# Stationary activation tiles moved to ten byte offsets against the streamed weights

## The chip, the core and the metric

One core of one Trainium2 chip runs the whole program. The metric is device time in microseconds (us), the median of several executions. The two activations and the products below run on the matrix engine (PE in the profile); its weight loads are shown apart, as PEld. DVE is the vector engine, ACT the scalar engine, POOL and SP two further engines; SP issues the transfers of the weights.

## What is computed

A decoder trunk of two layers on one sequence of 256 positions and width 2048, in float32. Layer 0 is sparse attention and a gated feed-forward, layer 1 a pooling mixer and a second gated feed-forward. The change touches the operands of three products: both down projections and the output product of the mixer.

```python
def pool_mixer(h, w_in, w_grp, scale, w_out):
    ...
    mixed = jnp.einsum('bsgc,gcd->bsgd', pooled, w_grp.astype(jnp.float32)).reshape(B, S, D)
    mixed = (mixed * scale.astype(jnp.float32)).astype(h.dtype)
    return mixed @ w_out

def swiglu(h, w_gu, w_down):
    gu = h @ w_gu
    gate, up = gu[..., :D_FF], gu[..., D_FF:]
    return (jax.nn.silu(gate) * up) @ w_down
```

D_FF is 5632, so a down projection has 44 blocks of 128 along its contraction; the mixer's output product has 16.

## The kernel before

Every float32 operand is kept as two parts, a rounded one and the rest. Weights arrive in blocks of 128 partitions by 1024 elements (`wraw`), in the order of one list, and ACT (L137) and DVE (L138) split each into `whi` and `wlo`; three buffers of each are in flight. An activation tile of 128 partitions holds 256 positions of the rounded part and 256 of the rest, side by side.

The large products are all made by `wide_gemm`. For each block k of the contraction, and each half t of the positions, it issues three matmuls. The activations `xa`, `xb` (128 by 128) are the stationary operand, loaded into the array by a weight load of its own, and 512 columns of `whi` or `wlo` are the moving operand:

```python
            for t in range(2):
                xa, xb = (rhs[k][:, a * S + t * P:a * S + (t + 1) * P] for a in range(2))
                nc.tensor.matmul(ps[t], xa, hi, start=k == 0, stop=False)
                nc.tensor.matmul(ps[t], xa, lo, start=False, stop=False)
                nc.tensor.matmul(ps[t], xb, hi, start=False, stop=k == n - 1)
```

These are lines 214 to 216. What the title of a row calls `acc<-whi,hid` is such a matmul: `whi` streams, `hid` stands in the array. The stationary tiles are `oT` (attention output, 16 tiles), `xg` (the normed input, 16), `hid` (the gated activation, 44, in 22 pairs, once in each feed-forward) and `mixed` (the mixer's, 16). A down projection runs four column blocks j, and in each of them all 44 blocks k in order.

In `ffn` the gate and up products alternate; ACT and DVE make `h` from them (L741, L745), PE transposes `h` (L752), and `split_pair` writes a pair of `hid` tiles (ACT L730, DVE L731). `mix_group` multiplies `pooled` by small weights and writes `mixed` (L815, L816). The weights' split waits for PE to free a buffer; nothing is ordered by hand around the change.

**Where the tiles lie.** Pools are stacked from the low end of the memory of a partition, their tiles one after another, each rounded up to a multiple of 32 bytes. The pool of `whi`, `wlo` and `wraw` begins 96 bytes past a multiple of 256, and its eleven buffers have 4096 bytes, so every streamed block lies at 96 modulo 256. `xg` follows directly: the same place. Between `xg` and the pool of the feed-forward lie 32 bytes for `rcol`, six times 32 for `na`, `nt` and `tot`, 32 for `ssq`, and tiles of 1024, 2048 and 16384 bytes: the small ones add up to 256, and `hid` lies at 96 again. In front of `mixed` lie tiles of 6144, 6144, 256 and eight times 4096 bytes: 96 too. `oT` is in a pool that is filled from the high end, and lies at 224, which is 128 bytes off the streamed blocks. In the text "off" is the place of a stationary tile minus that of the streamed one, modulo 256. The parts of a tile used by `wide_gemm` begin at multiples of 512 bytes in it, and those of a streamed block at 0 or 2048, so they add nothing to it.

Of the kernel before, what the change touches and what calls it, by code (L numbers as in the profile page):

```python
# [11 lines left out]
F32 = mybir.dt.float32  # L12
F32R = mybir.dt.float32r
# [4 lines left out]
P = 128  # L18
D = 2048
S = 256  # L20
KC = D // P
# [10 lines left out]
FT = DFF // P  # L32
# [35 lines left out]
def nsa_pool_trunk(ctx, tc, first, xn, small, band, gfin, w_qk, w_vg, w1k, w1v, w_o,  # L68
# [135 lines left out]
    def wide_gemm(rhs, own=False):  # L204

        ps = [bank(own) for _ in range(2)]
        n = len(rhs)
        for k in range(n):
            if k % 2 == 0:
                w = next_block()  # L210
            hi, lo = (a[:, k % 2 * N5:(k % 2 + 1) * N5] for a in w)
# [5 lines that stand above are left out]
        return ps  # L217
# [60 lines left out]
    at = ctx.enter_context(ExitStack())  # L278
# [17 lines left out]
    with tc.tile_pool(name="first", bufs=1, reuse_waits="tile") as fp, \  # L296
# [13 lines left out]
        for k in range(KC):  # L310
            n = wx[k].shape[1]
            o = KC + k * XW if k else 0
# [7 lines left out]
            for a, b in ((0, P), (P, F1)) if k == 0 else ((0, F1),):  # L320
                t = wx[k][:, n - F1 + a:n - F1 + b]
# [45 lines left out]
        f = rst.rearrange("p (c m j) -> p c m j", m=KQ, j=4)  # L367
# [13 lines left out]
        f = rst.rearrange("p (c i k) -> p i c k", i=CS // 2, k=2)  # L381
        for j in range(2):
            ps = ps1[3 + j].rearrange("p (c i k) -> p i c k", i=CS // 2, k=2)
            for g in range(2):
                a = slice(g * DV, (g + 1) * DV)
                o = (2 * j + g) * CS
# [17 lines left out]
        for br in range(2):  # L404
# [4 lines left out]
            for u in range(2):  # L409
                o = CS + u * S + br * P  # L410
# [240 lines left out]
    for q in range(NH // 4):  # L651
# [8 lines left out]
        for h in range(4 * q, 4 * q + 4, 2):  # L660
# [7 lines left out]
            o = oT[h // 2]  # L668
# [17 lines left out]
    def row_scale():  # L686

        tot = tmp.tile([P, 2], F32, name="tot")
        a = tmp.tile([P, 2], F32, name="na")
        t = tmp.tile([P, 2], F32, name="nt")  # L690
        nc.vector.tensor_reduce(tot, ssq, axis=AX.X, op=OP.add)
        nc.scalar.activation(t, tot, AF.Sqrt, scale=1.0 / D, bias=eps)
        nc.vector.tensor_scalar(a, tot, 1.0 / D, EPS, op0=OP.mult, op1=OP.add)
        nc.vector.reciprocal(rcol, t)
        nc.vector.scalar_tensor_tensor(t, rcol, -0.5, rcol, op0=OP.mult, op1=OP.mult)
        nc.vector.tensor_tensor(t, t, a, op=OP.mult)
        nc.vector.scalar_tensor_tensor(rcol, t, 1.5, rcol, op0=OP.add, op1=OP.mult)
# [22 lines left out]
            for i in range(2):  # L720
                spread(4 * j + 2 * q + i, tr[:, i * S:(i + 1) * S], gain)

    def pairs(pool, n, name):

        both = [pool.tile([P, 2, 2 * S], F32R, name=f"{name}{i}") for i in range(n // 2)]
        return both, [both[c // 2][:, c % 2] for c in range(n)]

    def split_pair(dst, tr):
# [1 line left out]
        nc.scalar.activation(dst[:, :, :S], src, AF.Copy)  # L730
        nc.vector.tensor_tensor(dst[:, :, S:], src, dst[:, :, :S].bitcast(F32), op=OP.subtract)  # L731

    def ffn(gain, fpool):
        hid2, hid = pairs(fpool, FT, "hid")
        for f in range(FJ):
            pg = wide_gemm(xg)
            if f == 0:
                row_scale()
            sg = [fpool.tile([P, N5], F32, name=f"sg{t}", bufs=1) for t in range(2)]
            for t in range(2):  # L740
                nc.scalar.activation(sg[t], pg[t], AF.Silu, scale=rcol[:, t:t + 1])  # L741
            pu = wide_gemm(xg)
            h = [fpool.tile([P, N5], F32, name="h", bufs=4) for t in range(2)]
            for t in range(2):
                nc.vector.scalar_tensor_tensor(h[t], pu[t], rcol[:, t:t + 1], sg[t], op0=OP.mult,  # L745
                                               op1=OP.mult)
            for q in range(2):
                tr = turn()
                for i in range(2):
                    for t in range(2):  # L750
                        o = (2 * q + i) * P
                        nc.tensor.transpose(tr[:, i * S + t * P:i * S + (t + 1) * P],  # L752
                                            h[t][:, o:o + P], ident)
                split_pair(hid2[2 * f + q], tr)
        gf = None
        if gain is None:
            gf = [fpool.tile([P, N5], F32, name="h", bufs=4) for _ in range(NJ)]
            for j in range(NJ):
                nc.sync.dma_start(gf[j], gfin[:, j * N5:(j + 1) * N5])
        for j in range(NJ):  # L760
            residual(j, wide_gemm(hid), gain, gf)
        return gf
# [3 lines left out]
    op.close()  # L766

    with tc.tile_pool(name="f0", bufs=1, reuse_waits="tile") as fpool:
        ffn("g_mix1", fpool)


    with tc.tile_pool(name="pl", bufs=1, reuse_waits="tile") as pl:

        raw = pl.tile([P, 4, 3 * P], F32, name="raw")
        bh = pl.tile([P, 4, 3 * P], F32R, name="bh")
        bl = pl.tile([P, 4, CS], F32R, name="bl")
        nc.sync.dma_start(raw, band)
        nc.gpsimd.tensor_copy(bh, raw)
        nc.gpsimd.tensor_tensor(bl, raw[:, :, :CS], bh[:, :, :CS].bitcast(F32), op=OP.subtract)
        pooled2, pooled = pairs(pl, KC, "pooled")  # L780
        mixed = [pl.tile([P, 2 * S], F32R, name=f"mixed{c}") for c in range(KC)]

        def pool_group(g, first):
            ps = wide_gemm(xg)
            if first:
                row_scale()
            uh = [pl.tile([P, N5], F32R, name=f"uh{t}", bufs=2) for t in range(2)]
            ul = [pl.tile([P, N5], F32R, name=f"ul{t}", bufs=2) for t in range(2)]
            for t in range(2):
                r = rcol[:, t:t + 1]  # L790
                nc.scalar.activation(uh[t], ps[t], AF.Copy, scale=r)
                nc.vector.scalar_tensor_tensor(ul[t], ps[t], r, uh[t].bitcast(F32), op0=OP.mult,
                                               op1=OP.subtract)
            for q in range(2):
                tr = turn()
                for i in range(2):
                    a = slice((2 * q + i) * P, (2 * q + i + 1) * P)
                    d = tr[:, i * S:(i + 1) * S]
                    nc.tensor.matmul(d, uh[0][:, a], bh[:, g, :S], start=True, stop=False)
                    nc.tensor.matmul(d, ul[0][:, a], bh[:, g, :S], start=False, stop=False)  # L800
                    nc.tensor.matmul(d[:, :CS], uh[0][:, a], bl[:, g], start=False, stop=False)
                    nc.tensor.matmul(d[:, P:], uh[1][:, a], bh[:, g, S:], start=False, stop=False)
                    nc.tensor.matmul(d[:, P:], ul[1][:, a], bh[:, g, S:], start=False, stop=True)
                split_pair(pooled2[2 * g + q], tr)

        def mix_group(g):
            for b in range(2):
                hi, lo = next_block()
                for j in range(2):
                    c = 4 * g + 2 * b + j  # L810
                    ps = bank()[:, :S]
                    for k in range(4):
                        o = (4 * j + k) * P
                        product(ps, hi[:, o:o + P], lo[:, o:o + P], pooled[4 * g + k], k == 0, k == 3)
                    nc.scalar.activation(mixed[c][:, :S], ps, AF.Copy, scale=col("scale", c))  # L815
                    nc.vector.scalar_tensor_tensor(mixed[c][:, S:], ps, col("scale", c),  # L816
                                                   mixed[c][:, :S].bitcast(F32), op0=OP.mult,
                                                   op1=OP.subtract)

        for i, g in enumerate(GROUPS):  # L820
            pool_group(g, i == 0)
            if i:
                mix_group(GROUPS[i - 1])
        mix_group(GROUPS[-1])
        rhs = [mixed[4 * g + c] for g in GROUPS for c in range(4)]
        for j in range(NJ):
            residual(j, wide_gemm(rhs), "g_ffn1")

    with tc.tile_pool(name="f1", bufs=1, reuse_waits="tile") as fpool:
        gf = ffn(None, fpool)  # L830
        row_scale()
        for j in (*range(NJ - 1), NJ - 1):
            for t in range(2):
                o = xs[:, t, j * N5:(j + 1) * N5]
                r = rcol[:, t:t + 1]
                if j == NJ - 1:
                    nc.vector.scalar_tensor_tensor(o, o, r, gf[j], op0=OP.mult, op1=OP.mult)
                elif t:
                    nc.scalar.activation(o, o, AF.Copy, scale=r)
                else:  # L840
                    nc.vector.tensor_scalar(o, o, r, None, op0=OP.mult)
                nc.sync.dma_start(out[t * P:(t + 1) * P, j * N5:(j + 1) * N5], o)
# [124 lines left out]
```

## Time and profile before

| | us |
|---|---|
| median of three runs | 2141.97 |
| lowest and highest | 2141.78, 2144.75 |
| the profiled execution | 2139.86 |
| span of its trace | 2137.7 |
| mean granted clock of PE, share of full speed | 0.997 |

The span runs from the first to the last instruction; the 2.2 us between it and the execution's time lie around it. All durations below come from this one execution, which is 2.1 us under the median. The page gives shares of the span by engine and a chain of the work that ended last; the other views are lists of groups of instructions, windows of time, and the instructions in order of time. Matmuls overlap in the pipeline, so the duration of one (some 390 ns) is more than what it adds: what counts here is the distance from the start of one matmul to the start of the next, called the pitch.

### The profile page before, as it was taken

The page shows a single profiled execution, that of the slowest core. Times are in us where ns is not written, and L with a number is a line of the kernel's source. Part 1 is how long each engine was busy: PE and PEld are TensorE (multiplying, and loading weights), DVE is VectorE, ACT ScalarE, POOL GpSimd, SP SyncE. Part 2 cuts the span into 40 slices and gives each one's busy share as a digit, 9 for nine tenths or more (in the row PEclk, how much of TensorE's full clock was granted, in tenths as well). Part 3 has the DMA queues.
Part 4 walks back from the last instruction along what each step waited for, and adds up shares of the span by engine and source line. Part 5 has one row for each costly group of instructions (what it writes and reads, how often), then busy time and mean ns, then how long its engine had stood idle before and what let it go on. Part 6 is the DMA issues. An engine that isn't in the chain of part 4 may idle for free.

```text
span 2137.7 us, 28134 instructions
## 1 busy us (share of the span) xinstructions
PE 2114.5 (99%) x10826; PEld 1807.7 (85%) x10826; DVE 1182.7 (55%) x1544; ACT 1036.8 (48%) x1491; POOL 53.2 (2%) x103
## 2 busy tenths in 40 slices
PE   8999999999999999999999999999999999999997
PEld 8999999888888888888888888888888888888886
DVE  7768888554554445544445555555444554444443
ACT  6567777454444444444444455444444444444443
POOL 1001111000000000000000000000000000000000
PEclk9999999999999999999999999999999999999999
DMA  6764444666666666666666655666666666666664
GB/s 231 216 211 136 150 141 132 198 183 191 191 184 195 188 190 193 183 193 188 196 189 190 197 177 178 187 188 187 190 191 189 189 187 193 189 208 194 193 193 127
DMA packets 113960, 396.92 MB, mean 186 GB/s; under 512 B 13314, under 2 KB 17538, under 8 KB 113570
## 3 DMA queue, kind: packets, MB, share of 16 engines
q1 hardware_dynamic: 113634, 394.80, 61.4%
q8 instruction: 85, 1.39, 0.3%
q10 hardware_dynamic: 192, 0.33, 0.1%
q14 instruction: 49, 0.40, 0.1%
HBM read 391.25 MB, written 2.16 MB: 184 GB/s over the span
## 4 chain that ended last, share of the span: by engine, by line
PE 93%; DVE 0%; ACT 0%; DVEq 0%; issue 0%
PE acc L214 27%; PE acc L215 27%; PE acc L216 27%; PE acc L169 2%; PE acc L171 2%; PE acc L170 2%; PE turn L752 1%; PE ps_o L645 1%; PE ps_t L607 1%; PE ps_s L541 1%; PE ps_s L539 1%; PE ps_s L540 1%; PE turn L718 0%; PE ps_o L636 0%; PE ps_o L635 0%; PE ps_o L637 0%
## 5 line engine op out<-in xcount | busy, mean ns | idle before, releaser
L138 DVE TENSOR_TENSOR wlo<-wraw,whi 128x1024 fp32r<-128x1024 f32 (+1 forms) x714 | 874.1, 1225 | 853.6 <-ACT whi L137 847.1
L137 ACT ACTIVATE whi<-wraw 128x1024 fp32r<-128x1024 f32 (+1 forms) x714 | 754.7, 1057 | 918.2 <-PE acc L216 849.9
L216 PE MATMUL acc<-whi,xg 128*128 128x512 f32 x1536 | 599.8, 390 | 0.0
L215 PE MATMUL acc<-wlo,xg 128*128 128x512 f32 x1536 | 598.3, 390 | 0.0
L214 PE MATMUL acc<-whi,xg 128*128 128x512 f32 x1536 | 545.8, 390 | 0.0
L215 PEld LDWEIGHTS acc<-wlo,xg 128*128 128x128 f32 x1536 | 288.4, 188 | 59.5
L216 PEld LDWEIGHTS acc<-whi,xg 128*128 128x128 f32 x1536 | 288.3, 188 | 59.1
L214 PEld LDWEIGHTS acc<-whi,xg 128*128 128x128 f32 x1536 | 288.4, 188 | 58.5
L215 PE MATMUL acc<-wlo,hid 128*128 128x512 f32 x704 | 274.2, 390 | 0.0
L216 PE MATMUL acc<-whi,hid 128*128 128x512 f32 x704 | 274.1, 389 | 0.0
L214 PE MATMUL acc<-whi,hid 128*128 128x512 f32 x704 | 247.5, 390 | 0.0
L214 PEld LDWEIGHTS acc<-whi,hid 128*128 128x128 f32 x704 | 132.1, 188 | 27.4
L216 PEld LDWEIGHTS acc<-whi,hid 128*128 128x128 f32 x704 | 132.1, 188 | 27.4
L215 PEld LDWEIGHTS acc<-wlo,hid 128*128 128x128 f32 x704 | 132.2, 188 | 27.2
L169 PE MATMUL acc<-xg,whi 128*128 128x256 f32 x464 | 131.8, 287 | 0.6 <-ACT whi L322 0.3
L170 PE MATMUL acc<-xg,whi 128*128 128x256 f32 x464 | 131.4, 286 | 0.0
L171 PE MATMUL acc<-xg,wlo 128*128 128x256 f32 x464 | 127.7, 285 | 0.0
L169 PEld LDWEIGHTS acc<-xg,whi 128*128 128x128 f32 x464 | 88.4, 191 | 1.2 <-ACT whi L322 0.6
L170 PEld LDWEIGHTS acc<-xg,whi 128*128 128x128 f32 x464 | 88.4, 190 | 0.2
L171 PEld LDWEIGHTS acc<-xg,wlo 128*128 128x128 f32 x464 | 86.4, 190 | 0.0
L567 ACT ACTIVATE prob<-prob,mx 128x128 f32<-128x128 f32 (+1 forms) x128 | 56.6, 445 | 9.8 <-DVE mx L561 6.8
L215 PE MATMUL acc<-wlo,oT 128*128 128x512 f32 x128 | 50.6, 395 | 0.0
(221 smaller groups left out, 1862.9 us busy)
## 6 DMA issues: line engine op xcount, KB each, us to landing
wraw<-in_gu SPq DMA_DIRECT2D x352, 512.0 KB, 3.6
wraw<-in_down SPq DMA_DIRECT2D x176, 512.0 KB, 3.7
wraw<-in_w_qk SPq DMA_DIRECT2D x60, 512.0 KB, 4.1
wraw<-in_w_o SPq DMA_DIRECT2D x32, 512.0 KB, 3.6
wraw<-in_p_in SPq DMA_DIRECT2D x32, 512.0 KB, 3.6
wraw<-in_p_out SPq DMA_DIRECT2D x32, 512.0 KB, 3.6
wx<-in_first SPq DMA_DIRECT2D x15, 448.0 KB, 8.9
bias<-skew SPq DMA_DIRECT2D x32, 200.0 KB, 3.3
```

Of the source, the lines that this page charges most:

```text
L137: nc.scalar.activation(hi[:, :n], t[:, :n], AF.Copy)
L138: nc.vector.tensor_tensor(lo[:, :n], t[:, :n], hi[:, :n].bitcast(F32), op=OP.subtract)
L169: nc.tensor.matmul(ps, hi, x[:, :S], start=first, stop=False)
L170: nc.tensor.matmul(ps, hi, x[:, S:], start=False, stop=False)
L171: nc.tensor.matmul(ps, lo, x[:, :S], start=False, stop=last)
L214: nc.tensor.matmul(ps[t], xa, hi, start=k == 0, stop=False)
L215: nc.tensor.matmul(ps[t], xa, lo, start=False, stop=False)
L216: nc.tensor.matmul(ps[t], xb, hi, start=False, stop=k == n - 1)
L539: nc.tensor.matmul(o, q[0], k[0], start=True, stop=False)
L540: nc.tensor.matmul(o, q[0], k[1], start=False, stop=False)
L541: nc.tensor.matmul(o, q[1], k[0], start=False, stop=True)
L567: nc.scalar.activation(p[:, o:o + n], p[:, o:o + n], AF.Exp, bias=mx[:, i:i + 1], accum_out=su[:, i:i + 1])
```

## The change

`pairs`, which allocates the tiles of `hid` and `pooled`, gets a list of wanted offsets in bytes. The pairs are cut into as many groups, in order of k. In front of a group a tile that nobody uses fills up multiples of 32 bytes; what is left under 32 bytes is made inside the tile, which then has 64 elements more. `mixed` gets 64 elements more in each tile and begins 1, 2, 12 or 60 elements into it.

- First feed-forward: `hid` at 64, 160, 192 and 224 bytes off, for 12, 10, 12 and 10 of the 44 blocks k.
- Mixer: `mixed` at 4, 8, 48 and 240 bytes off, four blocks k each.
- Second feed-forward: `hid` at 16 and 128 bytes off, 22 blocks k each.
- `pooled` gets no list and stays where it is. The tiles behind the padding move with it: `h` and `sg` by 224 bytes in the first feed-forward and by 128 (modulo 256) in the second.

No instruction is added or taken away; operands keep their shapes.

```diff
-    def pairs(pool, n, name):
-
-        both = [pool.tile([P, 2, 2 * S], F32R, name=f"{name}{i}") for i in range(n // 2)]
+    def pairs(pool, n, name, lines=()):
+
+
+        both, at = [], 0
+        for i in range(n // 2):
+            want = lines[i * len(lines) // (n // 2)] if lines else 0
+            if (want - at) % 256 // 32:
+                pool.tile([P, (want - at) % 256 // 32 * 8], F32, name=f"off{i}")
+                at = want // 32 * 32
+            fine = want % 32 // 4
+            t = pool.tile([P, 4 * S + (64 if fine else 0)], F32R, name=f"{name}{i}")
+            both.append(t[:, fine:fine + 4 * S].rearrange("p (c s) -> p c s", c=2))
         return both, [both[c // 2][:, c % 2] for c in range(n)]
...
-    def ffn(gain, fpool):
-        hid2, hid = pairs(fpool, FT, "hid")
+    def ffn(gain, fpool, lines):
+        hid2, hid = pairs(fpool, FT, "hid", lines)
...
-        ffn("g_mix1", fpool)
+        ffn("g_mix1", fpool, (64, 160, 192, 224))
...
-        mixed = [pl.tile([P, 2 * S], F32R, name=f"mixed{c}") for c in range(KC)]
+        mixed = [pl.tile([P, 2 * S + 64], F32R, name=f"mixed{c}") for c in range(KC)]
+        mixed = [t[:, o:o + 2 * S] for t, o in zip(mixed, (1,) * 4 + (2,) * 4 + (12,) * 4 + (60,) * 4)]
...
-        gf = ffn(None, fpool)
+        gf = ffn(None, fpool, (16, 128))
```

## Rows read from the trace of the kernel before

**Rows 1.** The page: busy time and share, then the chain that ended last.
```profile
PE 2114.5 (99%) x10826; PEld 1807.7 (85%) x10826; DVE 1182.7 (55%) x1544; ACT 1036.8 (48%) x1491; POOL 53.2 (2%) x103
...
PE 93%; DVE 0%; ACT 0%; DVEq 0%; issue 0%
```

**Rows 2.** Waits of PE, longest: line, releaser: us in total, times, longest.
```profile
PE acc L270 <- DVE rcol L267: 3.0, 1, 3.0
```

**Rows 3.** By tile (hid, mixed, oT): count, duration ns min/median/max, first and last start.
```profile
L214 PE MATMUL acc<-whi,hid x704: 387/389/483, 941.5 to 2123.3; 128*128 128x512 f32 x176
...
L730 ACT ACTIVATE hid<-turn x44: 592/596/599, 502.9 to 1890.2; 128x512 fp32r<-128x512 f32 x44
...
L214 PE MATMUL acc<-whi,mixed x128: 389/389/483, 1304.8 to 1394.0; 128*128 128x512 f32 x128
...
L214 PE MATMUL acc<-whi,oT x128: 390/393/497, 345.4 to 451.7; 128*128 128x512 f32 x128
```

**Rows 4.** Windows: stretch and length, busy us of each engine (instructions), PE clock, DMA share, GB/s.
```profile
414.00:434.00 20.00, 20.00 (x88) 16.21 (x87) 11.04 (x12) 9.19 (x13) 0.00 (x0) 1.00 0.61 176
481.00:501.00 20.00, 20.00 (x90) 16.53 (x90) 9.98 (x10) 8.28 (x8) 0.00 (x0) 1.00 0.67 194
1020.00:1040.00 20.00, 20.00 (x90) 16.57 (x89) 8.72 (x8) 8.22 (x8) 0.00 (x0) 1.00 0.67 189
1321.00:1331.00 10.00, 10.00 (x46) 8.29 (x45) 5.24 (x6) 5.47 (x8) 0.00 (x0) 1.00 0.62 176
```

**Rows 5.** Timeline of PE (start us, duration us): first and last instruction of three windows.
```profile
413.67 0.39 PE L216 MATMUL acc<-whi,oT 128*128 128x512 f32 x1
...
433.88 0.40 PE L216 MATMUL acc<-whi,oT 128*128 128x512 f32 x1
...
1019.76 0.39 PE L214 MATMUL acc<-whi,hid 128*128 128x512 f32 x1
...
1039.93 0.39 PE L214 MATMUL acc<-whi,hid 128*128 128x512 f32 x1
...
1320.68 0.39 PE L215 MATMUL acc<-wlo,mixed 128*128 128x512 f32 x1
...
1330.88 0.39 PE L215 MATMUL acc<-wlo,mixed 128*128 128x512 f32 x1
```

**Rows 6.** Timeline of PE: consecutive matmuls with oT standing.
```profile
416.93 0.39 PE L215 MATMUL acc<-wlo,oT 128*128 128x512 f32 x1
417.15 0.39 PE L216 MATMUL acc<-whi,oT 128*128 128x512 f32 x1
417.38 0.40 PE L214 MATMUL acc<-whi,oT 128*128 128x512 f32 x1
417.62 0.40 PE L215 MATMUL acc<-wlo,oT 128*128 128x512 f32 x1
417.86 0.40 PE L216 MATMUL acc<-whi,oT 128*128 128x512 f32 x1
```

**Rows 7.** Timeline of PE: xg standing, right behind the transposes that end at 458.24.
```profile
458.79 0.40 PE L214 MATMUL acc<-whi,xg 128*128 128x512 f32 x1
459.03 0.40 PE L215 MATMUL acc<-wlo,xg 128*128 128x512 f32 x1
...
461.55 0.39 PE L214 MATMUL acc<-whi,xg 128*128 128x512 f32 x1
461.78 0.39 PE L215 MATMUL acc<-wlo,xg 128*128 128x512 f32 x1
```

**Rows 8.** Timeline of PE, 256 columns: v0h or v0l standing, th or tl streaming.
```profile
228.37 0.28 PE L635 MATMUL ps_o<-th,v0h 128*128 128x256 f32 x1
...
229.31 0.28 PE L637 MATMUL ps_o<-th,v0l 128*128 128x256 f32 x1
```

**Rows 9.** Timeline of PE, 256 columns: whi or wlo standing, pooled streaming.
```profile
1262.01 0.28 PE L171 MATMUL acc<-pooled,wlo 128*128 128x256 f32 x1
...
1263.57 0.28 PE L171 MATMUL acc<-pooled,wlo 128*128 128x256 f32 x1
```

**Rows 10.** By line: transposes of xs (L718) and of h (L752).
```profile
L718 PE MATMUL turn<-ident,xs x96: 270/272/275, 387.0 to 1400.4; 128*128 128x128 f32 x96
...
L752 PE MATMUL turn<-ident,h x176: 270/272/275, 501.7 to 1889.7; 128*128 128x128 f32 x176
```

## Prediction

> **What bounds the kernel now.** I read the page first: PE is busy for 2114.5 of 2137.7 us, and the chain that ended last is PE's for 93%, with nothing of DVE or ACT in it that counts [rows 1]. Then the waits of PE: the longest is one of 3.0 us [rows 2]. So PE never waits for data in the three products that the change touches, and a change of layout can only count through how fast matmuls follow each other. Durations of matmuls don't tell that, since they overlap; the pitch does. I took it in stretches without transposes, from the first and last start in a window and the count of instructions in the window.
>
> - `oT` standing: 413.67 to 433.88 us with 88 matmuls, 20.21 / 87 = 232.3 ns [rows 4, 5].
> - `hid` standing: 1019.76 to 1039.93 us with 90, 20.17 / 89 = 226.6 ns [rows 4, 5].
> - `mixed` standing: 1320.68 to 1330.88 us with 46, 10.20 / 45 = 226.7 ns [rows 4, 5].
> - `xg`: also 90 in 20 us [rows 4].
>
> The instruction, its shape and PE's clock (1.00, so 2.4 GHz) are the same in all four. 512 columns at 2.4 GHz are 213.3 ns, so a matmul pays 13.3 ns on top with `xg`, `hid` and `mixed`, and 19.0 with `oT`. What differs by the program is the place: the first three lie 0 off the streamed weights, `oT` 128 off. This is the row on which everything rests: **a tile 128 bytes off costs 232.3 - 226.6 = 5.7 ns a matmul.** Two more views say how it comes. With `oT` the pitch never settles, it goes 0.22, 0.23, 0.24, 0.24 [rows 6]; with `xg` it is as uneven right behind a break (0.24) and then settles at 0.23 within some ten matmuls [rows 7]. The place 0 off thus seems to be one at which loads and streams fall into step, and the step is a cheap one.
>
> **The change part by part.** No instruction comes or goes. Of `hid`, three lines times 704 matmuls are touched, 2112; of `mixed` three times 128, 384 [rows 3]; 2496 in all. One block k has 4 x 2 x 3 = 24 matmuls. All of them are on the path that sets the end, with no cover: each ns of pitch counts in full.
>
> *Second feed-forward, 22 blocks at 128 off:* 22 x 24 = 528 matmuls. It is `oT`'s place, so 528 x 5.7 ns = 3.0 us.
>
> *First feed-forward, at 64, 160, 192 and 224 off:* 288, 240, 288 and 240 matmuls, 1056 in all. No stretch of the trace has 512 columns at these places. The bounds: from above, each pitch as long as the longest in [rows 6], 0.24 against 0.227, so 13 ns; from below, the shortest there, 0.22, so 7 ns less than now. That below nothing is not excluded is seen in 256-column matmuls: `v0h` and `v0l`, by the allocation 32 off what streams past them, have 0.94 us / 8 = 117.5 ns [rows 8], and weights that stand 0 off `pooled` have 1.56 / 13 = 120.0 [rows 9]. There, being off costs nothing and even saves 2.5 ns. I take the nearest row of the same shape, `oT`: 1056 x 5.7 = 6.0 us, with ends of -7 and +14 us.
>
> *Mixer at 4, 8, 48 and 240 off, and the other half of the second feed-forward at 16 off:* 384 + 528 = 912 matmuls. These lie within 48 bytes of place 0, which costs nothing more, so they stand between two rows: 0 and 5.7. I take the middle, 2.85: 912 x 2.85 = 2.6 us, with the same outer ends, -6 and +12 us.
>
> *Writers and transposes.* ACT's write of `hid` has 596 ns [rows 3] and DVE's like it; they run in engines that are busy for 48 and 55% [rows 1]. If misplaced writes took twice as long, the first product would still find its tile, since a down projection reads k in the order in which `ffn` wrote it and only the last pair is written just ahead of it. I cost them at nothing; without that cover one late pair per feed-forward costs about a write, 0.6 us. `h` moves too, to 224 and 128 off. `xs`, which is transposed in the same way from 224 off, has the same 272 ns as `h` [rows 10]: nothing. Padding adds no DMA and moves none in its queue. Behind each edge between two places some ten matmuls fall into a new step; at some 5 ns each, and 4 x (3 + 3 + 1) edges, that is 1.4 us if all had to; I leave it in the range.
>
> The sum is 3.0 + 6.0 + 2.6 = 11.6 us, on a span of 2137.7 and an execution of 2139.86: 2151.5. The median of runs is 2.1 us higher, so the forecast is 2153.6.
>
> **A rule that speaks against this.** The rows show that a pitch of the same shape differs with the stage by 5.7 ns [rows 4, 5]. The Trainium skill, page "TensorE: Matmul & The Clock Gate", section "Step-by-step: what each phase is for", says that PE has two independent read ports and that loading the next weights takes no read bandwidth from the running matmul. By it no place is better than another, and the sum would be 0. The trace does not bear it out: even 0 off, a matmul pays 13.3 ns over its columns.
>
> **The rivals.**
>
> 1. *Nothing changes.* The 5.7 ns of `oT` belong to its stage, not to its place, and loads and streams don't meet. For it: the 256-column rows, where being off is no dearer [rows 8, 9]; and that stretch has DVE busy for 11.0 of 20 us against 8.7 with `hid` [rows 4]. Against: `mixed` has DVE at 5.24 of 10 us, as busy, and the DMA share of `oT`'s stretch, and yet 226.7 ns [rows 4, 5]. Price 0: 2142. That the padding doesn't move what it means to move would give about the same: the places made inside the tiles, 4 to 240 and 16, stay, at 2.6 us or less. Chance 0.15.
> 2. *Faster.* The mechanism is the same falling into step, but at some places the step is shorter than 0 off's. The point from which it decides: the unknown 1968 matmuls must save more than the 3.0 us at 128 off cost, 1.5 ns each. For it: single pitches of 0.22 [rows 6] and the 256-column rows. Against: in 87 pitches with `oT` the short ones are paid back by 0.24s. At the 256-column gain of 2.5 ns, 1968 x 2.5 = 4.9 us less the 3.0: 2140. At 7 ns it is 13.8 less 3.0: 2131. Chance 0.07.
> 3. *Every place but 0 costs what 128 costs, also the near ones.* 2496 x 5.7 = 14.2 us: 2156. It differs from the forecast only in the near places and counts with it.
> 4. *Places that are no multiple of 16 or 32 bytes off cost far more*, since a load then touches more of the memory's lines. If 4, 8, 48, 240 and 16 took the longest pitch of [rows 6], 912 x 13 = 12 us in place of 2.6: 2163. Chance 0.08.
>
> **How the numbers follow.** Forecast with rival 3: 0.70, times from 2146.5 (only `oT`'s place and a third of the others pay) to 2158. Nothing changes 0.15, faster 0.07, far dearer 0.08. The range that leaves two in ten out reaches from 2142 to 2160. A measurement of this kernel tells some 0.2% from no change, 4.3 us: slower is over 2146.3, faster under 2137.7. Rival 2 is half within that band at its small price, so faster gets 0.04; same gets 0.15 from rival 1, 0.03 from rival 2 and 0.02 from the low end of the forecast, 0.20; slower 0.76.
>
> **What the profile after would show.** Windows of the second down projection's later half of each j: 88 instead of 90 matmuls in 20 us, and starts that step 0.22 to 0.24 as in [rows 6]. The first down projection: the same for most of its blocks; a group that stays at 90 has fallen into step at another place. The mixer's product: a pitch between 226.7 and 232. PE's waits, the counts of instructions, and the pitch with `xg` and `oT` stay. The prediction is wrong if the pitch at 128 off stays at 226.7 (then the stage, not the place, made `oT` slow), or if a group falls under 225.

## The result and the profile after

The changed kernel takes 2155.29 us, median of three runs (2153.01 to 2155.32), against 2141.97 before: a ratio of 1.0057, 95% interval 1.0042 to 1.0071. It is slower by more than the 0.2% that a measurement tells from no change. The profiled execution took 2153.01 us, 13.2 more than that of before, and its span is 2150.9.

The page, busy time by engine, and the longest wait of PE:

```profile
PE 2127.7 (99%) x10826; PEld 1810.3 (84%) x10826; DVE 1182.5 (55%) x1544; ACT 1036.9 (48%) x1491; POOL 52.7 (2%) x103
```
```profile
PE acc L270 <- DVE rcol L267: 3.0, 1, 3.0
```

These answer to [rows 1, 2]. The counts are the same, ACT and DVE are busy for as long as before, and PE still waits for nothing; but PE is busy for 13.2 us more. Where, is seen from the first and last start of a product's matmuls (columns as in [rows 3]). Before, the two down projections apart:

```profile
L214 PE MATMUL acc<-whi,hid x352: 387/389/483, 941.5 to 1183.9; 128*128 128x512 f32 x176
...
L214 PE MATMUL acc<-whi,hid x352: 387/389/477, 1883.7 to 2123.3; 128*128 128x512 f32 x176
```

And after: first down projection, the mixer's product, second down projection, then `oT` and, in two rows, the writes and transposes around `hid`:

```profile
L214 PE MATMUL acc<-whi,hid x352: 388/393/481, 942.8 to 1190.7; 128*128 128x512 f32 x176
...
L214 PE MATMUL acc<-whi,mixed x128: 388/392/483, 1311.6 to 1402.3; 128*128 128x512 f32 x128
...
L214 PE MATMUL acc<-whi,hid x352: 389/393/475, 1892.1 to 2136.4; 128*128 128x512 f32 x176
...
L214 PE MATMUL acc<-whi,oT x128: 390/393/498, 346.8 to 453.2; 128*128 128x512 f32 x128
...
L739 ACT ACTIVATE hid<-turn x44: 591/596/599, 504.4 to 1898.5; 128x512 fp32r<-128x512 f32 x44
...
L761 PE MATMUL turn<-ident,h x176: 270/272/273, 503.1 to 1898.1; 128*128 128x128 f32 x176
```

| product | before, us | after, us | difference | forecast |
|---|---|---|---|---|
| first down projection | 242.4 | 247.9 | 5.5 | 6.0 |
| mixer's product | 89.2 | 90.7 | 1.5 | 1.1 |
| second down projection | 239.6 | 244.3 | 4.7 | 4.5 |
| sum | | | 11.7 | 11.6 |

Of the 13.2 us between the two profiled executions, 11.7 lie in the three products. Another 1.4 us stand ahead of them: `oT`'s first matmul starts at 346.8 us, not 345.4 [rows 3]. No operand of that stretch moved, and in the runs below, most of which leave it as it was too, it ends between 344 and 348 us (347.2 in the run padded by 256, whose time is that of before): it differs from one execution to the next.

Inside the first down projection, second column block, the timeline shows the starts at the edges of three groups (160, 192 and 224 bytes off):

```profile
1022.45 0.39 PE L216 MATMUL acc<-whi,hid 128*128 128x512 f32 x1
...
1036.44 0.39 PE L216 MATMUL acc<-whi,hid 128*128 128x512 f32 x1
...
1052.92 0.39 PE L216 MATMUL acc<-whi,hid 128*128 128x512 f32 x1
...
1066.92 0.40 PE L216 MATMUL acc<-whi,hid 128*128 128x512 f32 x1
```

With 60, 72 and 60 matmuls between them the pitch is 13.99 / 60 = 233.2 ns at 160 off, 16.48 / 72 = 228.9 at 192, and 14.00 / 60 = 233.3 at 224. The mean over all starts that follow each other in the trace, breaks for transposes left out, gives for each place (a pitch is booked to the tile whose load runs beside the stream):

| off, bytes | 0 (`xg`) | 4 | 8 | 16 | 48 | 64 | 128 | 160 | 192 | 224 | 240 |
|---|---|---|---|---|---|---|---|---|---|---|---|
| pitch, ns | 226.9 | 232.3 | 230.7 | 230.1 | 233.5 | 233.3 | 232.4 | 233.3 | 228.9 | 233.3 | 227.5 |

Taken the same way, the three products had 226.8, 227.1 and 226.7 ns before. The differences, times the matmuls of each group, are 5.6, 1.5 and 4.8 us: the pitch explains the differences in the table above.

The 230.1 ns at 16 off are a mean of two pitches that stand apart. In the first and third column block of the second down projection the matmuls at 16 off settle at the 226.7 ns of 0 off, in the second and fourth at 233.3 ns, and they keep that for the rest of the 22 blocks k. First and last start of 60 pitches in the second column block, then in the third:

```profile
1970.14 0.39 PE L216 MATMUL acc<-whi,hid 128*128 128x512 f32 x1
...
1984.14 0.39 PE L216 MATMUL acc<-whi,hid 128*128 128x512 f32 x1
...
2031.15 0.39 PE L216 MATMUL acc<-whi,hid 128*128 128x512 f32 x1
...
2044.75 0.40 PE L216 MATMUL acc<-whi,hid 128*128 128x512 f32 x1
```

14.00 / 60 = 233.3 ns and 13.60 / 60 = 226.7. The tiles, their distance and the instructions are the same, and both column blocks begin behind matmuls at 128 off. So the distance narrows the pitch down, but at 16 off it leaves two; what decides between them, no run shows. At the other places the single steps differ, but in an order that repeats: 231 and 236 ns in turn at 64 off, 230, 232 and 238 at 160, 226, 229 and 232 at 192, and at 128, as with `oT` in the kernel before, a row of seven from 228 to 241.

### The profile page after: what moved, and what is told of

Read it like the earlier page. It is cut to its first block, busy times and chain, and to the rows that moved or that the text cites. A ratio compares the mean times of both kernels' runs of the same rounds, so it can differ in the third digit from the quotient of the medians.

```text
span 2150.9 us, 28134 instructions
## 1 busy us (share of the span) xinstructions
PE 2127.7 (99%) x10826; PEld 1810.3 (84%) x10826; DVE 1182.5 (55%) x1544; ACT 1036.9 (48%) x1491; POOL 52.7 (2%) x103
## 4 chain that ended last, share of the span: by engine, by line
PE 93%; DVE 0%; ACT 0%; DVEq 0%; issue 0%
PE acc L216 27%; PE acc L214 27%; PE acc L215 27%; PE acc L169 2%; PE acc L171 2%; PE acc L170 2%; PE turn L761 1%; PE ps_o L645 1%; PE ps_t L607 1%; PE ps_s L541 1%; PE ps_s L539 1%; PE ps_s L540 1%; PE turn L718 0%; PE ps_o L636 0%; PE ps_o L635 0%; PE ps_o L637 0%
## 5 line engine op out<-in xcount | busy, mean ns | idle before, releaser
L216 PE MATMUL acc<-whi,hid 128*128 128x512 f32 x704 | 277.5, 394 | 0.0
L214 PE MATMUL acc<-whi,hid 128*128 128x512 f32 x704 | 250.5, 394 | 0.0
```

## Experiments

My theory: the distance modulo 256 of the stationary tile to the streamed block sets the pitch, and 0 is a place where loads and streams fall into step. Rivals: the layout (padding, larger tiles, neighbours moved), the stage or layer, or the absolute place.

**Padding that moves nothing modulo 256.**

```diff
-                pool.tile([P, (want - at) % 256 // 32 * 8], F32, name=f"off{i}")
+                pool.tile([P, 64], F32, name=f"off{i}")
...
-            fine = want % 32 // 4
+            fine = 64 if want % 32 else 0
...
-        mixed = [t[:, o:o + 2 * S] for t, o in zip(mixed, (1,) * 4 + (2,) * 4 + (12,) * 4 + (60,) * 4)]
+        mixed = [t[:, o:o + 2 * S] for t, o in zip(mixed, (64,) * KC)]
```

> The changed kernel with every padding, outside and inside the tiles, made 256 bytes: the same tiles, enlarged or pushed apart, the neighbours moved, but every stationary tile 0 off again. If the place modulo 256 is the cause, hid and mixed are back at a pitch of 226.6 to 226.8 ns and the time is that of the kernel before, 2142 us, within 3. If padding, larger tiles or moved neighbours are the cause, it stays at 2153 to 2156 us.

Measured: 2141.43 us, ratio to before 0.9997 (0.9987 to 1.0006). The first down projection, with the padding in:

```profile
L214 PE MATMUL acc<-whi,hid x352: 387/389/483, 943.3 to 1185.8; 128*128 128x512 f32 x176
```

242.5 us, as before. Padding, larger tiles and moved neighbours cost nothing; the whole loss is the place modulo 256.

**All operands 128 bytes further, and all at 0.**

```diff
+    cst.tile([P, 32], F32, name="off")
     ident = cst.tile([P, P], F32, name="ident")
```

> The kernel before with 128 unused bytes ahead of the streamed blocks: whi, wlo, xg, hid and mixed all lie 128 bytes further (224 modulo 256), still 0 off each other, and oT, which is allotted from the other end and stays, comes to lie 0 off. If the distance to the streamed block decides, xg, hid and mixed keep 226.7 ns and oT falls from 232.3 to about 226.7: 384 matmuls by 5.7 ns, 2.2 us less than before, 2139.8 us. If the absolute place decides, oT keeps 232.3 and the others take the pitch that oT had, 232: 7100 matmuls by 5.7 ns, some 40 us more, 2180 us. If the stage and not the place made oT slow, nothing changes: 2142 us.

Measured: 2140.1 us, ratio 0.9995 (0.9986 to 1.0004). The gain is too small for the times, but the trace has it (`oT`, first and last start):

```profile
L214 PE MATMUL acc<-whi,oT x128: 389/389/497, 347.8 to 452.4; 128*128 128x512 f32 x128
```

104.6 us in place of 106.3 [rows 3]; by all starts the pitch of `oT` fell from 232.3 to 227.6 ns (226.7 where it has settled; the matmuls behind transposes take longer), those of `hid`, `mixed` and `xg` stayed to the tenth. `oT` did not move in the memory: what it streams moved. So the distance decides whether the pitch is that of 0 off, not the absolute place and not the stage. The rival that the dear rows of `oT` belonged to its stage is out.

```diff
+    cst.tile([P, 40], F32, name="off")
     ident = cst.tile([P, P], F32, name="ident")
...
+    o_pool.tile([P, 56], F32, name="offT")
     hp = at.enter_context(tc.tile_pool(name="hp", bufs=2, reuse_waits="tile"))
```

> The kernel before with streamed blocks, xg, hid, mixed and oT all at 0 modulo 256, 0 off each other. If only the distance decides, as in the run that moved all by 128: hid, mixed and xg at 226.7 ns, oT at 227.6, 2140 us. If the absolute place modulo 64 or 32 plays a part (it was 32 modulo 64 until now), all pitches change together, and with 7488 matmuls 1 ns is 7.5 us: outside 2137 to 2143 us.

Measured: 2140.22 us, ratio 0.9993 (0.9984 to 1.0003), `oT` 227.6 ns and the others within 0.1 of before. With 0 off the absolute place modulo 64 plays no part either. The distances other than 0 were tried with `whi` at one place, 96 modulo 256, only; that they too are independent of the absolute place is not shown.

**Twenty-six groups.** Each group's padding and start inside the tile were made to fit, for the places in the text:

```diff
-        ffn("g_mix1", fpool, (64, 160, 192, 224))
+        ffn("g_mix1", fpool, (32, 96, 80, 112, 144, 176, 208, 240, 252, 248, 128))
...
-        gf = ffn(None, fpool, (16, 128))
+        gf = ffn(None, fpool, (12, 24, 188, 196, 200, 212, 216, 232, 236, 244, 64))
...
-        mixed = [t[:, o:o + 2 * S] for t, o in zip(mixed, (1,) * 4 + (2,) * 4 + (12,) * 4 + (60,) * 4)]
+        mixed = [t[:, o:o + 2 * S] for t, o in zip(mixed, (60,) * 4 + (48,) * 4 + (32,) * 4 + (16,) * 4)]
```

> The changed kernel with other places: first feed-forward 32, 96, 80, 112, 144, 176, 208, 240, 252, 248 and 128 bytes off (four blocks k each, 96 matmuls), second 12, 24, 188, 196, 200, 212, 216, 232, 236, 244 and 64, mixer 240, 192, 128 and 64. If the place decides, those that were tried in another product keep their pitch there: 128 some 232.4 ns, 64 some 233.2, 192 some 228.9, 240 some 227.5, each within 1. If the product or layer decides, the first feed-forward's groups would all be near 233 but one, and the mixer's between 227 and 233 in the order of before. Of the new places none is expected below 226.5 (chance 0.25 that one is); mean over all near 231, time 2152 us, from 2149 to 2157.

Measured, 2154.63 us:

| off | 12 | 24 | 32 | 64 | 80 | 96 | 112 | 128 | 144 | 176 | 188 |
|---|---|---|---|---|---|---|---|---|---|---|---|
| ns | 231.7 | 231.1 | 233.3 | 233.3, 233.4 | 232.1 | 234.2 | 233.4 | 233.3, 232.2 | 233.3 | 230.4 | 232.9 |

| off | 192 | 196 | 200 | 208 | 212 | 216 | 232 | 236 | 240 | 244 | 248 | 252 |
|---|---|---|---|---|---|---|---|---|---|---|---|---|
| ns | 229.4 | 233.3 | 231.1 | 231.7 | 236.2 | 232.1 | 230.7 | 231.7 | 228.3, 228.3 | 233.1 | 233.0 | 233.3 |

Places tried in another product keep their pitch within 1 ns (64, 128, 192, 240). At 12 off there are two, as at 16: 226.7 ns in the first column block and 233.1 in the other three. The two values at 128 belong to two rows of steps as well, 229 and 238 ns in turn in the first feed-forward and the row of seven in the mixer. A group has only 24 matmuls in a column block, and the first of them are still settling, so a difference of a few tenths says nothing about the place. The mean is higher than I expected, nearer 232 than 231. No place is better than 0, and being near it is no safe help: 252, four bytes short of 0, has 233.3 in all four column blocks. At 112 off the pitch is as steady as at 0, only longer:

```profile
1023.62 0.39 PE L215 MATMUL acc<-wlo,hid 128*128 128x512 f32 x1
1023.85 0.39 PE L216 MATMUL acc<-whi,hid 128*128 128x512 f32 x1
1024.09 0.39 PE L215 MATMUL acc<-wlo,hid 128*128 128x512 f32 x1
1024.32 0.39 PE L216 MATMUL acc<-whi,hid 128*128 128x512 f32 x1
1024.55 0.39 PE L214 MATMUL acc<-whi,hid 128*128 128x512 f32 x1
1024.79 0.39 PE L215 MATMUL acc<-wlo,hid 128*128 128x512 f32 x1
```

Steps of 0.23, 0.24, 0.23, 0.23, 0.24; by all starts the group has 233.4 ns. So there are at least two steady steps, 226.7 and 233.3 ns, 13.3 and 20.0 over the 213.3 of 512 columns, 6.7 apart; elsewhere unequal steps repeat, with a mean between or above the two.

**Does a tile off its place cost its neighbours?** The first 32 blocks of `hid` at 0 and 64 off in turn:

```diff
+            if n == FT and i < 16:
+                t = pool.tile([P, 4 * S + 64], F32R, name=f"{name}{i}")[:, :4 * S + 32]
+                both.append(t.rearrange("p (c s) -> p c s", c=2)[:, :, :2 * S])
...
```

> The kernel before with hid at 0 and 64 bytes off in turn, block by block, for the first 32 of 44 blocks k in both down projections; the last 12 at 0. If each matmul pays for its own place, those blocks have the mean of 226.7 and 233.3, 230.0 ns: 1536 by 3.3 ns, 5 us, 2147 us. If a tile off its place breaks the step for its neighbours, all of them are near 233 and the time is 2152 us. The last 12 blocks come back to 226.7 in either case.

Measured: 2149.2 us, between the two. In those blocks the pitch, booked as in the table of places, is 233.1 ns where a tile 64 off is loaded and 230.9 where one 0 off is; the last 12 blocks are at 227.1. So a tile at its place pays some 4 ns of a neighbour's fault. The steps of the timeline differ, 0.23, 0.24 and 0.23 here and from 225 to 236 ns by all starts, and settle on neither 226.7 nor 233.3:

```profile
1015.70 0.39 PE L214 MATMUL acc<-whi,hid 128*128 128x512 f32 x1
1015.93 0.40 PE L215 MATMUL acc<-wlo,hid 128*128 128x512 f32 x1
1016.17 0.39 PE L216 MATMUL acc<-whi,hid 128*128 128x512 f32 x1
1016.40 0.62 PE L214 MATMUL acc<-whi,hid 128*128 128x512 f32 x2
```

**One streamed part off its place.**

```diff
-        lo = wp.tile([P, BLK], F32R, name="wlo", bufs=SPL)
+        lo = wp.tile([P, BLK + 64], F32R, name="wlo", bufs=SPL)[:, 32:32 + BLK]
...
```

> The kernel before with wlo alone moved 128 bytes further in its buffers; whi, xg, hid and mixed stay 0 off each other. One in three matmuls now streams a block that the stationary tiles are 128 off. If each matmul pays for its own pair alone, the two that stream whi keep 226.7 ns and the one that streams wlo pays 5.7 more: some 2400 by 5.7 ns, 14 us, 2156 us. If what 0 off gives is a step that three equal distances in a row keep up, all three become uneven, near 232: 7100 by 5.7 ns, 40 us, 2182 us.

Measured: 2162.34 us, some 20 over before, again between the two expectations. Here a pitch is booked to the matmul that streams. Of the matmuls with `xg`, those that stream `whi`, 0 off, take 229.0 ns and those that stream `wlo` 232.0; with `hid` the order is turned round, 231.0 and 230.1. Booked to the load beside the stream, as in the tables above, `xg` too has `whi` dearer, 230.7 against 228.6. Mean over all 230.2. That the matmuls whose own pair is 0 off pay as well is shown; how the price is shared out was not foreseen, and the order depends on the booking.

**Half the load.** Only the second of three matmuls with 64 stationary columns, then, by the same edit in all three lines, all of them (blocks 1 to 42):

```diff
-                nc.tensor.matmul(ps[t], xa, lo, start=False, stop=False)
+                nc.tensor.matmul(ps[t][:half], xa[:, :half], lo, start=False, stop=False)
...
```

> The kernel before with half of the stationary columns (64 of 128) in the second of the three matmuls in both down projections; the rest's product is left out for the other 64 positions of each half. The streamed columns stay 512. If the weight load takes its time out of the stream that runs beside it, the pitch of the matmul ahead of it falls from 226.7 towards 220 ns (half of the 13.3 ns gone), the others stay: 704 by 6.7 ns, up to 4.7 us less, 2137 us. If the 13.3 ns are a fixed price per matmul, all pitches stay at 226.7 and the time at 2142 us.

> The kernel before with 64 of 128 stationary columns in all three matmuls of blocks k 1 to 42 of both down projections (the product for the other 64 positions is left out there). All loads are equal and half as long; the streams stay at 512 columns. If equal loads 0 off fall into step and the 13.3 ns are the load's own time taken from the stream, the pitch settles at 220 ns: 2016 by 6.7 ns, 13 us less, 2129 us. If they fall into step but the price is fixed, 226.7 and 2142 us. If half loads don't fall into step at 0 off, uneven pitches near 230 as in the run with one half load: 2149 us.

Measured: 2149.21 and 2148.56 us, both slower than before with less work. The pitch in the down projections is 230.3 ns in the first and 229.9 in the second, 0 off. In the second:

```profile
1015.22 0.40 PE L216 MATMUL acc<-wlo,hid 128*64 128x512 f32 x1
1015.46 0.39 PE L217 MATMUL acc<-whi,hid 128*64 128x512 f32 x1
1015.69 0.40 PE L215 MATMUL acc<-whi,hid 128*64 128x512 f32 x1
1015.92 0.39 PE L216 MATMUL acc<-wlo,hid 128*64 128x512 f32 x1
1016.15 0.39 PE L217 MATMUL acc<-whi,hid 128*64 128x512 f32 x1
1016.38 0.39 PE L215 MATMUL acc<-whi,hid 128*64 128x512 f32 x1
1016.60 0.40 PE L216 MATMUL acc<-wlo,hid 128*64 128x512 f32 x1
```

0.24, 0.23, 0.23, 0.23, 0.23, 0.22; by all starts six steps from 224 to 236 ns repeat. Neither expectation of the first run came true, and of the second run's the third did: half loads 0 off don't fall into the even step. Both theories of the first run, the load's own time taken from the stream and a fixed price per matmul, had supposed that they do, so these runs don't decide between them; what the 13.3 ns consist of stays open. Shown is that 0 off, the cheapest place for a full load of 128 columns beside 512 streamed ones, gives half a load no even step.

**So what of other shapes?** [rows 8, 9] had said that with 256 columns 0 off is not the best. There the small weight blocks stand and `xg` streams; they were put at twelve places off `xg`, one after another, in the kernel that moves all by 128 bytes:

```diff
-            blocks(w[j], P, sizes)
+            blocks(w[j], P, sizes, (0, 32, 64, 96, 128, 160, 192, 224, 16, 240, 48, 8)[j % 12])
...
-        hi = wp.tile([P, BLK], F32R, name="whi", bufs=SPL)
+        hi = wp.tile([P, BLK + 64], F32R, name="whi", bufs=SPL)[:, off // 4:off // 4 + BLK]
...
```

> The kernel with all moved by 128 bytes, and the small weight blocks of the query and key products, which there are the stationary operand against 256 streamed columns of xg, at twelve places off xg, one after another: 0, 32, 64, 96, 128, 160, 192, 224, 16, 240, 48, 8. At 0 the pitch is 119.3 ns in the kernel before (106.7 for 256 columns, 12.6 on top). If 0 off is the best place whatever is streamed, all others are at 119.3 or above and the time is at or over 2140 us. If, as the matmuls with v0h standing 32 off had it (117.5), the best place depends on how many columns stream, some are near 117.5: at 2 ns and some 1400 matmuls the best place for all would be worth 2.8 us.

Measured: 2138.43 us. In the query products, of some 85 pitches each:

| off | 0 | 8 | 16 | 32 | 48 | 64 | 96 | 128 | 160 | 192 | 224 | 240 |
|---|---|---|---|---|---|---|---|---|---|---|---|---|
| ns | 119.5 | 116.7 | 118.4 | 118.3 | 120.0 | 114.3 | 118.2 | 118.9 | 119.6 | 118.3 | 117.1 | 118.4 |

Here 0 is one of the dearest. A second scan with neighbours of the best, by the same edit:

> As the first scan of the small blocks, with the places 64, 60, 68, 72, 56, 80, 4, 112, 88, 8, 208 and 144. 64 is expected again at 114.3 ns within 1 and 8 at 116.7 within 1, in other tiles than before; if the pitch belongs to the tile and its neighbours rather than the place, they are not. The neighbours of 64 (60, 68, 56, 72) are expected between 114 and 118, none under 113.5.

Measured: 2137.26 us. 64 again 114.8 ns, in other tiles; 8 was 117.9, 1.2 off its first value; 4, 56, 60, 68 and 72 had 118.4, 118.1, 119.7, 118.4 and 118.6, above what I had expected of the neighbours of 64; 80, 88, 112, 144 and 208 had 118.6, 115.7, 119.6, 119.5 and 116.7. The best place is a narrow one.

**A version from it:** large products 0 off, small blocks 64 off.

```diff
-            blocks(w[j], P, sizes)
+            blocks(w[j], P, sizes, 64)
...
-            blocks(p_grp[GROUPS[i - 1]], BLK, (1, 1))
+            blocks(p_grp[GROUPS[i - 1]], BLK, (1, 1), 64)
...
```

> All large products 0 off (as in the run that moved all by 128), and every small weight block that stands against 256 streamed columns 64 bytes off, the best of the twelve places scanned (114.3 ns against 119.4 at 0). About 1392 matmuls with xg and 192 with pooled: if each saves 5 ns, 7.9 us on 2140.1, 2132 us; if only those in the query products save it and the early ones 1 ns, 6.4 us, 2134 us. If the place has no lasting effect there because other work of the attention stage fills the time, 2140 us. Against the kernel before: a ratio of 0.995 to 0.997.

Measured: 2135.62 us, ratio to before 0.9969 (0.9958 to 0.9981): faster than the kernel before, and the interval does not overlap that of the kernel with all moved by 128 bytes (0.9986 to 1.0004). It is at the weak end of what I expected. Means by all starts: query products 115.3 ns (119.3 before), `pooled` 115.2 (119.8), early products 118.1 (117.1): in the early ones, where I had expected 1 ns, nothing was won. Where it settles, the step is 113.3 ns; before, in the same product:

```profile
119.51 0.28 PE L169 MATMUL acc<-xg,whi 128*128 128x256 f32 x1
...
122.75 0.28 PE L169 MATMUL acc<-xg,whi 128*128 128x256 f32 x1
```

and in this version:

```profile
120.31 0.28 PE L169 MATMUL acc<-xg,whi 128*128 128x256 f32 x1
...
123.03 0.28 PE L169 MATMUL acc<-xg,whi 128*128 128x256 f32 x1
```

27 matmuls in 3.24 us are 120.0 ns, 24 in 2.72 us are 113.3: again 6.7 apart, and 13.3 and 6.7 over the 106.7 of 256 columns. In the attention stage other matmuls come between, and the step has to be found anew, so the mean stays 2 ns over it.

## Why the prediction was right, and where it was not

The forecast was 2153.6 us; 2155.29 was measured. The trace gave 11.7 us in the three products against 11.6. Which way the time moves, how it comes about and the size of the largest terms were right; that the sum agrees to 0.1 us is luck, since one term was 0.7 too low and another 0.5 too high.

- *What bounds the kernel.* Right: no wait appeared, and PE's busy time rose by the whole difference.
- *`oT`'s 5.7 ns are the place's.* Right, shown by the run that moved what `oT` streams. The term from it, 528 matmuls at 128 off, has the same pitch here, 232.4 ns: 3.0 us as forecast. That the pitch with `oT` "never settles" is not right: its steps repeat in a row of seven, and so they do at 128 off.
- *Between 64 and 224 off, 5.7 ns each.* Right in the sum, 5.5 measured for 6.0. By single places it is 6.6 at 64, 160 and 224, and 2.2 at 192: the row I took was the right size, but a place has a price of its own that a neighbour's doesn't tell.
- *Near 0 stands between 0 and 5.7.* Wrong as a rule. The places within 48 bytes pay 5.6 (4 off), 4.0 (8), 6.8 (48) and 0.8 (240); 16 off pays nothing in two column blocks and 6.7 in the other two, 3.4 in the mean. Against the pitches of before, the 912 matmuls cost 1.8 us at 16 off and 1.5 in the mixer, 3.3 for the 2.6 forecast, 3.6 ns each for 2.85; the cheaper 192 made it good. This is the mis-sized term, and the reason given for it does not hold: 4 bytes are enough to lose the step. That 16 off comes near the forecast's 2.85 is luck too: the middle of two rows was taken for a price, while each column block has either the one step or the other. The sign that the prediction named for a group that has "fallen into step at another place", 90 matmuls in 20 us, came there, from 2024 to 2044 us. Rival 3, every place at 5.7, fails by the same numbers.
- *Nothing for writers, transposes and padding.* Right: ACT's write has 596 ns and the transposes of `h` 272, as in [rows 3, 10], and the run padded by 256 is not slower. DVE's write, said to be like ACT's, has 686 ns, before and after.
- *Groups' edges, up to 1.4 us.* Not seen as a cost of its own: the groups' pitches, edges included, give the measured sum.
- *Faster.* The point from which it decides was not reached: none of the 512-column places tried lies under 226.7 ns. Its argument, that 256 columns are cheaper off 0, was sound for 256 columns, and the small blocks' version shows it; it did not carry over to 512.
- *The rule that speaks against the change*, in the Trainium skill's page "TensorE: Matmul & The Clock Gate", section "Step-by-step: what each phase is for", that a load takes no read bandwidth from the running matmul, would have given 0. The same instructions with their operands 0 to 252 bytes off take from 226.7 to 236.2 ns here, with 0 off the fastest, so where the load reads and where the stream reads do bear on each other; through what, no run shows.

Open is why 0 off is best with 512 columns and 64 off with 256, why the settled steps lie 6.7 ns apart, and what decides between the two at 12 and 16 off.

## What to carry to other kernels

Where PE is busy all the time and each matmul brings its own load, read the pitch from the starts, stage by stage: two stages of the same shape with different pitches point to where their operands lie, which the durations of the instructions hardly show. Read it by column block too, before taking a mean: 230.1 ns at 16 off was 226.7 in two of them and 233.3 in two. Place all stationary tiles at the one distance modulo 256 that the shape likes best, found by a scan of groups in one kernel, and scan again for each streamed width: here, of the places tried, 0 for 512 columns and 64 for 256. A single operand off its place costs its neighbours too, and tiles behind small odd ones in a pool lose or keep the place by chance.

## What the runs showed of the hardware that I had not expected

Less load made it slower: 64 stationary columns in place of 128 raised the pitch from 226.7 to some 230 ns. Settled pitches were 113.3 and 120.0 ns with 256 columns, 226.7 and 233.3 with 512, all 6.7 or a multiple of it over the columns' own time at 2.4 GHz (at 0 off, 256 columns more take 226.7 - 120.0 = 106.7 ns more, which is 256 at 2.4 GHz). The same 22 tiles at the same 16 bytes off ran at 226.7 ns in one column block and at 233.3 in the next. And four bytes between two operands cost 5.6 ns a matmul, as much as 128.
